# The attention loop of a hybrid transformer kernel: from the scheduler's order to a written order on four engines

## The chip, the cores and the metric

One core of a Trainium2 chip. The metric is device time of one execution in microseconds (us); a lower time is better. The engines are PE (matmuls; PEld is its weight load), DVE (vector), ACT (scalar, activations), POOL (GpSimd) and SP, which here only issues DMAs. Each engine works through its own queue of instructions in order and waits there, by semaphores, for the others.

## The reference, cut to what matters

Two layers of a hybrid backbone over 1,024 latent tokens and 256 context tokens of width 1,024. In each layer a normed input is projected once, the columns are split into attention heads, mLSTM heads and a pooling mixer, and the concatenation goes through one output projection; then a SwiGLU follows. The part that matters here is the attention: 8 query heads of 64, 2 key/value heads.

```python
def block_attention(q, k, v):
    ...
    def one_block(qi):                      # 128 queries
        s = jnp.einsum('bqhgd,bkhd->bhgqk', qi, k, preferred_element_type=F32) * scale
        p = jax.nn.softmax(s, -1).astype(v.dtype)
        return jnp.einsum('bhgqk,bkhd->bqhgd', p, v)
...
att_l = block_attention(q_l, jnp.concatenate([k_l, k_c], 1), jnp.concatenate([v_l, v_c], 1))
...
xl = xl + g1_l * (jnp.concatenate([att_l, ml_l, pool_l], -1) @ w_out)
```

In the first layer the 256 context tokens attend too, to themselves alone. All of it is 32-bit float.

## The kernel before

To keep 32-bit accuracy on 16-bit matmuls, an operand is split into an fp16 part and the fp16 remainder, and a product is three matmuls (`TERMS`). A split is an ACT copy and a subtraction on DVE or POOL.

The attention of a layer is a list of units. A unit is one head of one block of 128 queries against 1,280 keys; the blocks of context queries (first layer, two of them) have units of four heads against 256 keys. There are 68 units in layer 0 and 64 in layer 1. A unit passes through three methods:

- `front`: the scores, six matmuls into a tile `Sp` of three PSUM banks (there are two such tiles); the row maximum (`mx`, L1315, DVE); its scaling (L1320, or L1322 and L1323 for context units); the exponential on ACT into `pf` (two buffers), which also adds up the row's sum.
- `split`: the fp16 copy of `pf` into `phl` (three buffers), on ACT, in every eighth unit on DVE (L1334); the remainder on POOL (L169, the helper `tt`); the transpose of both by one DMA into `pT` (five buffers, L1340).
- `values`, for a pair of heads, that is two units: the reciprocal of the sums (L1351, DVE); two fp32 matmuls that spread it over the columns of a PSUM bank (L1354); an ACT copy of that into SBUF (`u`, tile `ao`); 60 value matmuls into other columns of the same bank (L1361); the scaling on DVE back into `ao`; an ACT copy to the fp16 part of `mixT` and a DVE subtraction for its remainder.

The loop (L1437) writes, in round i, `front` of unit i, `split` of unit i-1, at most one fill, and from round 5 on the values of units i-5 and i-4 where a pair begins; then `pump` takes one step of any running thread, such as a norm. A fill is a piece of the output projection: `w_get` brings a weight tile (the `w_split` inside it makes the split of the next tile: `hl`, an ACT copy and a DVE remainder), 12 matmuls for 256 or 512 tokens go into a PSUM bank (`wout`, L1372), and DVE adds the scaled result to `X`. `w_get` is called once for each of 24 weight tiles of a layer in the loop, and the tile serves one to three blocks of tokens. A budget decides when a fill is written: each round adds `pace`, a fill costs its tokens over 200.

```python
            if i >= 3:
                budget = min(budget + pace(i / nu), 3.0)
                if budget > 0:
                    c = next(fill, None)
                    if c is None:
                        c = next(fill_ffn, 0)
                    budget -= c
```

This text is not the order in which the engines run. A scheduler takes the instructions with their data dependencies, plays them through with costs of its own, and puts each on its engine's queue when it finds it ready; earlier text has the higher priority. Order edges that carry no semaphore can be added by `tc.add_manual_dep(..., order)`: the kernel does so for its activations, so that the table of functions is not switched back and forth (`after`), and for successive maxima (`tabs["mx"]`). PSUM in this stage is two `Sp` tiles of three banks and two single banks (`bank`), which the value pairs, the fills and the norms share in turn. The helpers `act` (L152), `stt` (L166) and `tt` (L169) issue most of the ACT, DVE and POOL work, so that rows carry their lines.

Of the kernel before, what the change touches and what calls it, by code (L numbers as in the profile page):

```python
# [9 lines left out]
F32 = mybir.dt.float32  # L10
# [8 lines left out]
P = 128  # L19
# [61 lines left out]
@with_exitstack  # L81
def hybrid_kernel(ctx: ExitStack, tc: tile.TileContext, I, out, dbg=None):
    nc = tc.nc
    V, S, G, TE, DMA = nc.vector, nc.scalar, nc.gpsimd, nc.tensor, nc.sync
    MUL, ADD, SUB, MAX, MIN = ALU.mult, ALU.add, ALU.subtract, ALU.max, ALU.min
    dbg = dbg or {}

# [33 lines left out]
    def bank3(name="S"):  # L121
        return cur["s"].tile([P, 1536], F32, tag="S", name=name)
# [5 lines left out]
    def pt_(shape, dt, tag, bufs=1, name=None):  # L128
        return cur["w"].tile(list(shape), dt, tag=tag, name=name or tag, bufs=bufs)

    def f2k(shape=(P, 512), dt=F32, name="f2k"):
        return pt_(shape, dt, "f2k", F2K[cur["kind"]], name)


    mm = TE.matmul
    order = mybir.DependencyInfo(mybir.DependencyClass.NoSync, mybir.DependencyReason.DATA)
    tabs = {"last": [], "pre": None, "kind": None}

    def after(i, j):
# [28 lines left out]
    def tt(o, a, b, op, e=None):  # L168
        (e or V).tensor_tensor(o, a, b, op=op)  # L169
# [354 lines left out]
    class Sums:  # L524


        def __init__(self, t0, n):
            self.t0, self.n, self.acc, self.k = t0, n, [], 0
# [212 lines left out]
    for l in range(DEPTH):  # L741
# [465 lines left out]
        for (t0, n) in BLOCKS:  # L1207
            if t0 in nx:
                drain(nx.pop(t0))
            for r in range(3):  # L1210
# [4 lines left out]
                else:  # L1215
                    pb = bank("pfm")
# [80 lines left out]
        class Unit:  # L1297
# [4 lines left out]

            def front(self):
                qt, nk, k0, n = self.qt, self.nk, self.k0, self.n
                Sp = bank3("Sp")
                for e, h in enumerate(self.hs):
                    ql = qkv[:, h // 2, h % 2, qt * P:(qt + 1) * P]
                    for a in range(2):
                        for b0 in range(0, nk, 512):
                            m = min(512, nk - b0)  # L1310
                            mm(Sp[:, e * nk + b0:e * nk + b0 + m], ql, qkv[:, 4 + h // 4, a, k0 + b0:k0 + b0 + m],  # L1311
                               start=(a == 0), stop=(a == 1), skip_group_check=True)
                ne = len(self.hs)
                mx = pt_((P, 4), F32, "mx", 3)
                r = V.tensor_reduce(mx[:, :ne], Sp[:, :n].rearrange("p (e k) -> p e k", e=ne), axis=AX.X, op=MAX)  # L1315
                if "mx" in tabs:
                    after(r.ins, tabs["mx"])
                h0 = self.hs[0]
                if ne == 1:
                    tabs["mx"] = V.tensor_scalar(mx[:, :1], mx[:, :1], rq[:, 1, qt, h0:h0 + 1], LN4096, op0=MUL, op1=ADD).ins  # L1320
                else:
                    tt(mx[:, :ne], mx[:, :ne], rq[:, 1, qt, h0:h0 + ne], MUL)  # L1322
                    tabs["mx"] = V.tensor_scalar(mx[:, :ne], mx[:, :ne], LN4096, None, op0=ADD).ins  # L1323
                self.pf = pt_((P, NTOK), F32, "pf", PFB)
                for e, h in enumerate(self.hs):
                    act(self.pf[:, e * nk:(e + 1) * nk], Sp[:, e * nk:(e + 1) * nk], AF.Exp, bias=mx[:, e:e + 1],
                        scale=rq[:, 0, qt, h:h + 1],
                        accum_out=self.qs[1][:, h:h + 1])

            def split(self):  # L1330
                i, n, pf = self.i, self.n, self.pf
                hl = pt_((P, 2, NTOK), F16, "phl", PHB)
                if i % 8 == 0:
                    V.tensor_copy(hl[:, 0, :n], pf[:, :n])  # L1334
                else:
                    act(hl[:, 0, :n], pf[:, :n])
                tt(hl[:, 1, :n], pf[:, :n], hl[:, 0, :n], SUB, G)
                self.pT = pt_((P, 2, 10, P), F16, "pT", PTB)
                if n == NTOK:
                    DMA.dma_start_transpose(out=self.pT.rearrange("p a k c -> p (a k) c"), in_=hl.rearrange("p a t -> p (a t)"))  # L1340
                else:
                    for a in range(2):
                        DMA.dma_start_transpose(out=self.pT[:, a, :n // P], in_=hl[:, a, :n])

        def values(us, pair):

            qt, sums = us[0].qt, us[0].qs[1]
            nkt, k0 = us[0].nk // P, us[0].k0
            hs = (2 * pair, 2 * pair + 1)
            kv = pair // 2  # L1350
            V.reciprocal(sums[:, hs[0]:hs[0] + 2], sums[:, hs[0]:hs[0] + 2])  # L1351
            pb = bank("pv")
            for g, h in enumerate(hs):
                mm(pb[64 * g:64 * g + 64, P:2 * P], sums[:, h:h + 1].to_broadcast([P, 64]), idn, start=True, stop=True)  # L1354
            u = f2k((P, 2, P), F32, "ao")
            act(u[:, 0], pb[:, P:2 * P])
            for kt in range(nkt):
                for j, (a, b) in enumerate(TERMS):
                    for g, h in enumerate(hs):
                        un = us[g if len(us) == 2 else 0]  # L1360
                        mm(pb[64 * g:64 * g + 64, 0:P], qkv[:, 6, b, k0 + kt * P:k0 + (kt + 1) * P][:, kv * 64:kv * 64 + 64],  # L1361
                           un.pT[:, a, un.hs.index(h) * nkt + kt], start=(kt == 0 and j == 0), stop=(kt == nkt - 1 and j == 2),
                           skip_group_check=True)
            tt(u[:, 1], pb[:, 0:P], u[:, 0], MUL)
            q = slice(qt * P, (qt + 1) * P)
            act(mixT[:, pair, 0, q], u[:, 1])
            tt(mixT[:, pair, 1, q], u[:, 1], mixT[:, pair, 0, q], SUB)

        def wout(w, k0, m, t0, n, pb):
            for k in range(4):  # L1370
# [62 lines left out]
        def pace(part):  # L1433

            return (1.1 if part < 0.9 else 2.5) if last else 0.8 if part < 0.2 else 1.5

        for i in range(nu + 5):  # L1437
            now[0] = i
            if i < nu:
                units[i].front()  # L1440
            if 1 <= i <= nu:
                units[i - 1].split()
            if i >= 3:
                budget = min(budget + pace(i / nu), 3.0)
                if budget > 0:
                    c = next(fill, None)
                    if c is None:
                        c = next(fill_ffn, 0)
                    budget -= c
            if i >= 5:  # L1450
                u = units[i - 5]
                if len(u.hs) > 1:
                    for e in range(0, len(u.hs), 2):
                        values([u], u.hs[e] // 2)
                elif u.hs[0] % 2 == 0:
                    values([u, units[i - 4]], u.hs[0] // 2)
                if u.hs[-1] in (6, 7) and u.qt < 8:
                    done[0] = u.qt
                units[i - 5] = u = None
            pump()  # L1460
        for _ in fill:
            pass
        units = fill = None
# [544 lines left out]
```

## Time and profile before

| | us |
|---|---|
| median of 3 runs | 2874.22 |
| lowest, highest | 2868.87, 2874.91 |
| the profiled execution | 2869.33 |
| its span, first to last instruction | 2867.5 |
| attention loop of layer 0, first score matmul to last exponential | about 373 to 704 |
| attention loop of layer 1 | about 1872 to 2160 |

The profile is one execution. An engine's busy time is the union of its instructions, and matmuls overlap each other, so that six matmuls of 0.4 us take 1.25 us together. A row's number in square brackets is the idle time of the engine ahead of it and what ended it. `issue` stands where nothing the profile shows was waited for. PEclk 1.00 is the full TensorE clock.

### The profile page before, as it was taken

How to read it: one execution, taken by the hardware profiler on the slowest of the kernel's cores; microseconds unless marked ns; L12 is line 12 of the kernel's file. 1: busy time of each engine (PE TensorE's matmuls, PEld its weight loads, DVE VectorE, ACT ScalarE, POOL GpSimd, SP SyncE). 2: the span in 40 equal slices, each digit the busy share in tenths (PEclk: the TensorE clock that was granted, in tenths of full speed). 3: DMA queues.
4: the chain of work that ended last, by engine and by line, in shares of the span. 5: the costliest groups of instructions: out<-in, count | busy, mean ns of one | idle time of the engine just before them, and what ended most of it. 6: DMA issues, size and time to landing. Idle time of an engine off the chain costs nothing. (4 is left out here: it accounts for less than half of the span.)

```text
span 2867.5 us, 54408 instructions
## 1 busy us (share of the span) xinstructions
PE 2601.2 (91%) x21619; PEld 1502.1 (52%) x21619; DVE 1951.8 (68%) x3379; ACT 1407.4 (49%) x2776; POOL 1283.6 (45%) x979
## 2 busy tenths in 40 slices
PE   7999978887889999999999998878877799999997
PEld 4875554555545555555554684544455344444444
DVE  5458867668766565656665567877778776666666
ACT  5345556666534343434344544466765444444453
POOL 1123445566434443444443213455664554555551
PEclk9999989999999999999999999999998899999999
DMA  9534487888122222222212212498984111111211
GB/s 291 151 108 128 134 191 141 154 149 171 52 74 82 81 89 89 82 81 89 74 45 76 67 53 68 123 173 160 171 168 106 45 59 52 59 59 45 67 52 74
DMA packets 631636, 296.28 MB, mean 103 GB/s; under 512 B 362888, under 2 KB 620756, under 8 KB 630868
## 3 DMA queue, kind: packets, MB, share of 16 engines
q1 hardware_dynamic: 631204, 292.73, 41.3%
q8 instruction: 169, 2.77, 0.4%
q14 instruction: 87, 0.71, 0.1%
q10 hardware_dynamic: 176, 0.07, 0.0%
HBM read 176.19 MB, written 20.87 MB: 69 GB/s over the span
## 5 line engine op out<-in xcount | busy, mean ns | idle before, releaser
L1903 PEld LDWEIGHTS <-hlp 128*128 128x128 f16 x5040 | 492.7, 98 | 609.7 <-issue 36.6
L1903 PE MATMUL Swb<-T,hlp 128*128 128x512 f16 x1920 | 446.2, 382 | 28.3 <-ACT T L152 14.3
L169 POOL TENSOR_TENSOR phl<-pf,phl 128x1280 f16<-128x1280 f32 (+1 forms) x132 | 345.2, 2617 | 260.9 <-ACT phl L152 160.3
L166 DVE SCALAR_TENSOR_TENSOR hlp<-ws,hlp 128x512 f16<-128x512 f32 (+1 forms) x320 | 235.2, 741 | 150.7 <-ACT hlp L152 116.7
L152 ACT ACTIVATE hlp<-ws 128x512 f16<-128x512 f32 (+1 forms) x320 | 163.7, 518 | 217.8 <-PE Swb L1903 86.7
L152 ACT ACTIVATE pf<-Sp,mx,rq 128x1280 f32<-128x1280 f32 (+1 forms) x144 | 189.8, 1320 | 142.1 <-DVE mx L1320 115.4
L1311 PE MATMUL Sp<-T 128*128 128x512 f16 (+1 forms) x800 | 180.9, 357 | 71.3 <-ACT pf L152 69.1
L1903 PE MATMUL Swc<-T,hlp 128*128 128x512 f16 x960 | 227.2, 379 | 0.0
L1903 PE MATMUL Swb<-tq,hlp 128*128 128x512 f16 x960 | 220.5, 379 | 4.9 <-ACT T L152 4.7
L1315 DVE TENSOR_REDUCE mx<-Sp 128x1 f32<-128x1280 f32 (+1 forms) x132 | 194.4, 1473 | 34.4 <-PE Sp L1311 34.0
L1372 PE MATMUL pwo<-T,hl 128*128 128x512 f16 (+1 forms) x960 | 190.6, 345 | 29.8 <-DVE X L166 11.6
L466 PE MATMUL pfm<-T,hl 128*128 128x512 f16 (+1 forms) x1032 | 213.6, 360 | 4.2 <-ACT E L152 4.1
L152 ACT ACTIVATE T<-sg 128x512 f16<-128x512 f32 (+1 forms) x170 | 100.2, 600 | 234.1 <-POOL sg L169 155.7
L166 DVE SCALAR_TENSOR_TENSOR hlp<-st,hlp 128x256 f16<-128x256 f32 (+1 forms) x201 | 142.5, 713 | 87.5 <-ACT hlp L152 73.0
L1915 PE MATMUL dx<-T,hlp 128*128 128x256 f16 x1440 | 177.9, 273 | 12.2 <-DVE hlp L166 6.4
L169 POOL TENSOR_TENSOR ws<-st 128x256 f32<-128x256 f32 (+1 forms) x97 | 103.0, 1069 | 183.5 <-DMA st<-in_w_ffn_down_dram 74.9
L169 POOL TENSOR_TENSOR X<-X,T 128x512 f32<-128x512 f32 x80 | 112.7, 1409 | 151.0 <-DVE X L166 112.2
L1903 PE MATMUL Swa<-T,hlp 128*128 128x512 f16 x720 | 169.1, 380 | 0.0
L1915 PEld LDWEIGHTS <-hlp 128*128 128x128 f16 x1440 | 139.2, 100 | 44.7 <-issue 10.8
L1361 PEld LDWEIGHTS <-T 128*64 128x64 f16 x3936 | 128.4, 119 | 56.4 <-issue 56.0
L152 ACT ACTIVATE hlp<-st 128x256 f16<-128x256 f32 (+1 forms) x201 | 101.3, 510 | 113.9 <-PE Swb L1903 71.1
L1361 PE MATMUL pv<-pT,T 128*64 128x128 f16 x3936 | 137.3, 233 | 17.6 <-ACT ao L152 17.5
(323 smaller groups left out, 4827.9 us busy)
## 6 DMA issues: line engine op xcount, KB each, us to landing
T<-in_w_ada_dram SPq DMA_DIRECT2D x48, 512.0 KB
rawa<-in_w_ada_dram SPq DMA_DIRECT2D x48, 512.0 KB
st<-in_w_in_dram SPq DMA_DIRECT2D x32, 512.0 KB
st<-in_w_out_dram SPq DMA_DIRECT2D x64, 256.0 KB
st<-in_w_ffn_gate_dram SPq DMA_DIRECT2D x32, 512.0 KB
st<-in_w_ffn_up_dram SPq DMA_DIRECT2D x30, 512.0 KB
st<-in_w_ffn_down_dram SPq DMA_DIRECT2D x30, 512.0 KB
xs<-X SPq DMA_DIRECT2D x4, 2048.0 KB
```

Source lines behind the costliest of these rows:

```text
L152: b = S.activation(o, i, f, **kw).ins
L166: V.scalar_tensor_tensor(o, a, s, b, op0=o0, op1=o1)
L169: (e or V).tensor_tensor(o, a, b, op=op)
L466: mm(o, w[:, a, k, :], h[:, k, b, t0:t0 + n], start=(k == 0 and j == 0), stop=(k == nk - 1 and j == 2))
L1311: mm(Sp[:, e * nk + b0:e * nk + b0 + m], ql, qkv[:, 4 + h // 4, a, k0 + b0:k0 + b0 + m], start=(a == 0), stop=(a == 1), skip_group_check=True)
L1315: r = V.tensor_reduce(mx[:, :ne], Sp[:, :n].rearrange("p (e k) -> p e k", e=ne), axis=AX.X, op=MAX)
L1361: mm(pb[64 * g:64 * g + 64, 0:P], qkv[:, 6, b, k0 + kt * P:k0 + (kt + 1) * P][:, kv * 64:kv * 64 + 64], un.pT[:, a, un.hs.index(h) * nkt + ...
L1372: mm(pb, w[:, a, k, :], mixT[:, k0 + k, b, t0:t0 + n], start=(k == 0 and j == 0), stop=(k == 3 and j == 2))
L1903: mm(o, w[:, a, k, :], B[:, b], start=(s in "172" and k == 0 and j == 0), stop=(k == kh(i) - 1 and j == 2), skip_group_check=True)
L1915: mm(dbank[i][:, r * 256:(r + 1) * 256], w[:, a, k, :], B[:, b], start=(first and k == 0 and j == 0), stop=(not first and k == kh(i) - 1 a ...
```

## The change

The engines of vector, scalar, GpSimd and tensor are wrapped in a class that, between `in_row(True)` and `in_row(False)`, adds an order edge from each instruction to the one written before it on the same engine. The loop runs inside that stretch, so its four queues have the order of the text; SP's queue has not. The text of a round is rewritten: values of units i-6 and i-5 come first, up to their matmuls; then `split` of unit i-1; then the scaling of these values; then `front` and the new `exps` of unit i; then fills, as many as the budget gives (it may grow to 4), but in a round with values only while it is above 2. The scaled values go to a third column range of the pair's PSUM bank instead of SBUF, and the two parts of `mixT` are made from there. All fp16 copies of `pf` are on ACT.

```diff
+    class InRow:
...
+            def call(*a, **k):
+                b = f(*a, **k)
+                if row["on"]:
+                    if self.key in row:
+                        tc.add_manual_dep(b.ins, row[self.key].name, order, reason="written order")
+                    row[self.key] = b.ins
+                return b
...
+    V, S, G, TE = (InRow(e, k) for k, e in enumerate((nc.vector, nc.scalar, nc.gpsimd, nc.tensor)))
...
+            def exps(self):
+                nk, qt, mx, Sp = self.nk, self.qt, self.mx, self.Sp
                 self.pf = pt_((P, NTOK), F32, "pf", PFB)
...
-                if i % 8 == 0:
-                    V.tensor_copy(hl[:, 0, :n], pf[:, :n])
-                else:
-                    act(hl[:, 0, :n], pf[:, :n])
+                act(hl[:, 0, :n], pf[:, :n])
...
-            u = f2k((P, 2, P), F32, "ao")
-            act(u[:, 0], pb[:, P:2 * P])
+            u = f2k((P, P), F32, "ao")
+            act(u, pb[:, P:2 * P])
...
-            tt(u[:, 1], pb[:, 0:P], u[:, 0], MUL)
+            yield
+            o = pb[:, 2 * P:3 * P]
+            tt(o, pb[:, 0:P], u, MUL)
             q = slice(qt * P, (qt + 1) * P)
-            act(mixT[:, pair, 0, q], u[:, 1])
-            tt(mixT[:, pair, 1, q], u[:, 1], mixT[:, pair, 0, q], SUB)
+            act(mixT[:, pair, 0, q], o)
+            tt(mixT[:, pair, 1, q], o, mixT[:, pair, 0, q], SUB)
...
-        for i in range(nu + 5):
+        in_row(True)
+        for i in range(nu + 6):
             now[0] = i
+            vals = []
+            if i >= 6:
+                u = units[i - 6]
+                if len(u.hs) > 1:
+                    vals = [values([u], h // 2) for h in u.hs[::2]]
+                elif u.hs[0] % 2 == 0:
+                    vals = [values([u, units[i - 5]], u.hs[0] // 2)]
...
+            for g in vals:
+                next(g)
+            if 1 <= i <= nu:
+                units[i - 1].split()
+            for g in vals:
+                next(g, None)
             if i < nu:
                 units[i].front()
-            if 1 <= i <= nu:
-                units[i - 1].split()
+            if i < nu:
+                units[i].exps()
             if i >= 3:
-                budget = min(budget + pace(i / nu), 3.0)
-                if budget > 0:
+                budget = min(budget + pace(i / nu), 4.0)
+                while budget > (2.0 if vals and i < nu else 0):
                     c = next(fill, None)
                     if c is None:
                         c = next(fill_ffn, 0)
+                    if not c:
+                        break
                     budget -= c
-            if i >= 5:
...
             pump()
+        in_row(False)
```

## Rows read from the trace of the kernel before

**Rows 1.** The page's parts 1 and 2: engines; DMA share in tenths by slice.

```profile
PE 2601.2 (91%) x21619; PEld 1502.1 (52%) x21619; DVE 1951.8 (68%) x3379; ACT 1407.4 (49%) x2776; POOL 1283.6 (45%) x979
...
DMA  9534487888122222222212212498984111111211
```

**Rows 2.** Windows, value rounds of the two loops, all engines.

```profile
core 0: us, PE busy (x) PEld busy (x) DVE busy (x) ACT busy (x) POOL busy (x), PEclk, DMA share, GB/s
395.40:705.00 309.60, 251.16 (x2914) 156.74 (x2913) 227.08 (x327) 198.53 (x331) 181.45 (x80) 0.94 0.83 154
1896.30:2160.00 263.70, 211.41 (x2533) 127.10 (x2530) 200.60 (x263) 177.19 (x264) 163.67 (x68) 0.94 0.91 168
```

**Rows 3.** The same windows, row maximum (L1315) alone.

```profile
395.40:705.00 309.60, 90.68 (x62) 0.94 0.83 154
1896.30:2160.00 263.70, 84.43 (x57) 0.94 0.91 168
```

**Rows 4.** Waits, layer 1 window: waiter, releaser, us, times, longest.

```profile
ACT pf L152 <- DVE mx L1320: 48.9, 20, 4.7
...
PE Sp L1311 <- ACT pf L152: 37.6, 24, 4.9
```

**Rows 5.** Tile ao, whole run: ns min/median/max; then who waited.

```profile
L169 DVE TENSOR_TENSOR T<-ao,T x72: 274/859/2667, 397.8 to 2178.6; 128x128 f16<-128x128 f32 x72
...
  PE pv L1361: 17.5, 20
```

**Rows 6.** Timeline, layer 1, 2020 to 2042 us: start, duration, instructions.

```profile
2022.85 0.44 PE L1354 MATMUL pv<-idn,sums 128*64 128x128 f32 x4
...
2023.22 0.93 PE L1311 MATMUL Sp<-T 128*128 128x512 f16 x4
...
2024.65 0.27 ACT L152 ACTIVATE ao<-pv 128x128 f32<-128x128 f32 x1
...
2024.96 1.87 PE L1361 MATMUL pv<-pT,T 128*64 128x128 f16 x60 [0.81 <-ACT ao L152]
...
2028.90 0.21 DVE L1320 TENSOR_SCALAR mx<-mx,rq 128x1 f32<-128x1 f32 x1
...
2029.23 1.42 ACT L152 ACTIVATE pf<-Sp,mx,rq 128x1280 f32<-128x1280 f32 x1 [1.65 <-DVE mx L1320]
...
2030.77 1.27 ACT L152 ACTIVATE phl<-pf 128x1280 f16<-128x1280 f32 x1
...
2037.78 2.62 POOL L169 TENSOR_TENSOR phl<-pf,phl 128x1280 f16<-128x1280 f32 x1 [0.27 <-POOL phl L169]
2038.08 2.47 DVE L169 TENSOR_TENSOR T<-ao,T 128x128 f16<-128x128 f32 x1
...
2038.36 1.25 PE L1311 MATMUL Sp<-T 128*128 128x512 f16 x6
```

**Rows 7.** Tile hl, 1896 to 2160 us.

```profile
L152 ACT ACTIVATE hl<-st x21: 612/618/630, 1910.6 to 2157.2; 128x512 f16<-128x512 f32 x21
L166 DVE SCALAR_TENSOR_TENSOR hl<-st,hl x20: 671/1399/3161, 1911.3 to 2157.7; 128x512 f16<-128x512 f32 x20
```

**Rows 8.** Tile X, 1896 to 2160 us.

```profile
L166 DVE SCALAR_TENSOR_TENSOR X<-pwo,prm,X x28: 467/739/751, 1897.9 to 2158.3; 128x512 f32<-128x512 f32 x22, 128x256 f32<-128x256 f32 x6
```

**Rows 9.** Line L1351, whole run.

```profile
L1351 DVE RECIPROCAL sums<-sums x72: 148/165/168, 380.4 to 2165.5; 128x2 f32<-128x2 f32 x72
```

**Rows 10.** Windows, two falls of the granted clock, before and behind each.

```profile
592.00:595.70 3.70, 0.80 (x8) 0.31 (x7) 3.61 (x6) 2.19 (x5) 0.36 (x1) 1.00 0.74 164
595.70:599.00 3.30, 3.30 (x61) 3.15 (x60) 0.17 (x1) 3.30 (x5) 2.22 (x1) 0.50 0.54 99
2086.00:2090.70 4.70, 0.33 (x2) 0.19 (x2) 3.32 (x8) 2.37 (x4) 1.32 (x2) 1.00 1.22 179
2090.70:2094.00 3.30, 3.30 (x11) 1.34 (x9) 3.30 (x3) 1.13 (x2) 2.30 (x1) 0.50 0.36 107
```

**Rows 11.** Timeline, layer 0, 511 to 520 us.

```profile
514.24 3.24 PE L1361 MATMUL pv<-pT,T 128*64 128x128 f16 x60 [1.74 <-ACT ao L152]
```

More of the change, by code (lines that the diff above doesn't have):

```diff
@@ L83, in hybrid_kernel, with __init__, __getattr__, in_row @@
     nc = tc.nc
-    V, S, G, TE, DMA = nc.vector, nc.scalar, nc.gpsimd, nc.tensor, nc.sync
+    order = mybir.DependencyInfo(mybir.DependencyClass.NoSync, mybir.DependencyReason.DATA)
+    row = {"on": False}
+    class InRow:
+        def __init__(self, e, key):
+            self.e, self.key = e, key
+        def __getattr__(self, name):
+            f = getattr(self.e, name)
+            def call(*a, **k):
[5 more added lines that the diff above has]
+                return b
+            return call
+    def in_row(on):
+        row.clear()
+        row["on"] = on
+    V, S, G, TE = (InRow(e, k) for k, e in enumerate((nc.vector, nc.scalar, nc.gpsimd, nc.tensor)))
+    DMA = nc.sync
     MUL, ADD, SUB, MAX, MIN = ALU.mult, ALU.add, ALU.subtract, ALU.max, ALU.min
@@ L135, in hybrid_kernel @@
     mm = TE.matmul
-    order = mybir.DependencyInfo(mybir.DependencyClass.NoSync, mybir.DependencyReason.DATA)
     tabs = {"last": [], "pre": None, "kind": None}
@@ L1304, in front @@
                 qt, nk, k0, n = self.qt, self.nk, self.k0, self.n
-                Sp = bank3("Sp")
+                Sp = self.Sp = bank3("Sp")
                 for e, h in enumerate(self.hs):
@@ L1323, in front @@
                     tabs["mx"] = V.tensor_scalar(mx[:, :ne], mx[:, :ne], LN4096, None, op0=ADD).ins
+                self.mx = mx
+            def exps(self):
+                nk, qt, mx, Sp = self.nk, self.qt, self.mx, self.Sp
                 self.pf = pt_((P, NTOK), F32, "pf", PFB)
+                self.mx = self.Sp = None
                 for e, h in enumerate(self.hs):
@@ L1435, in pace @@
             return (1.1 if part < 0.9 else 2.5) if last else 0.8 if part < 0.2 else 1.5
-        for i in range(nu + 5):
+        in_row(True)
+        for i in range(nu + 6):
             now[0] = i
+            vals = []
[5 more added lines that the diff above has]
+                    vals = [values([u, units[i - 5]], u.hs[0] // 2)]
+                if u.hs[-1] in (6, 7) and u.qt < 8:
+                    done[0] = u.qt
+                units[i - 6] = u = None
+            for g in vals:
[4 more added lines that the diff above has]
+                next(g, None)
             if i < nu:
                 units[i].front()
-            if 1 <= i <= nu:
-                units[i - 1].split()
+            if i < nu:
+                units[i].exps()
             if i >= 3:
-                budget = min(budget + pace(i / nu), 3.0)
-                if budget > 0:
+                budget = min(budget + pace(i / nu), 4.0)
+                while budget > (2.0 if vals and i < nu else 0):
                     c = next(fill, None)
@@ L1448, in hybrid_kernel @@
                         c = next(fill_ffn, 0)
+                    if not c:
+                        break
                     budget -= c
-            if i >= 5:
[L1451 to L1459, printed above, removed]
             pump()
+        in_row(False)
         for _ in fill:
```

## The prediction

> **What bounds the kernel now.** I read the page's first two parts first [rows 1]: PE is busy 91% of the span, but in slices 6 to 10 and 27 to 30 of the forty, where the two attention loops lie, the DMA row stands at 7 to 9 and is low almost everywhere else. The rest of the program is not touched, so the argument is about those two stretches. Next the windows of the two loops [rows 2], taken from the round at which values begin: 309.6 us in layer 0 and 263.7 us in layer 1. No engine is full there: PE 81% and 80%, DVE 73% and 76%, ACT 64% and 67%, POOL 59% and 62%; the DMA engines, with the transposes of the probabilities, are at 0.83 and 0.91. The row-maximum line counted in the same windows gives the pace [rows 3]: 62 units in 309.6 us and 57 in 263.7 us. As two units make a head pair with one `values`, that is 31 pairs at 9.99 us and 28.5 pairs at 9.25 us. Third, who waits for whom [rows 4]: the exponentials (`pf`) wait 48.9 us for the scaled maximum, and `Sp` waits 37.6 us for exponentials. So the loop is bound by nothing single; it is a ring of waits PE, DVE, ACT, which the scheduler loosens by letting PE run one or two score tiles ahead of the values.
>
> **What the new order fixes.** A round with values runs, on each engine in this order: reciprocal (DVE), two broadcasts (PE), copy `u` (ACT), 60 value matmuls (PE); fp16 copy of unit i-1 (ACT), its remainder (POOL), transpose; scaling (DVE), two parts of `mixT` (ACT, DVE); scores of unit i (PE), maximum and its scaling (DVE), exponential (ACT); then fills. The next round has no values.
>
> Three of these edges close a ring. The value matmuls wait for `u`, which lies in the same bank: 20 times PE idled until it was done, 17.5 us in all [rows 5]; one is shown, `u` at 2024.65, matmuls at 2024.96 [rows 6]. The scores of unit i now stand behind those matmuls on PE. And `u` stands behind the previous round's exponential on ACT. Before, scores ran first: 2023.22 ahead of 2024.96 [rows 6].
>
> **The ring for one pair, step by step** (from the timeline [rows 6]; the maximum is 84.43 us over 57 [rows 3]):
> - `u` 0.27, 60 value matmuls 1.87, six score matmuls 1.25, maximum 1.48, scaling 0.21, exponential with its accumulator read 1.54 (it starts at 2029.23, the next ACT instruction at 2030.77): 6.62 us;
> - next round: fp16 copy 1.27, exponential 1.54 (its scores and maximum ran meanwhile): 2.81 us;
> - hand-overs between engines as the timeline shows them, 0.03 to 0.12 us each: 0.42 us.
>
> That is 9.85 us. 31 pairs make 305 us against 309.6 (-4), 28.5 make 281 against 263.7 (+17): together **+13 us**. The first six rounds, where the loads of `X` dominate, and what follows the loop I leave as they are.
>
> **Weight tiles.** `w_get` in a fill emits, behind the round's exponential, an fp16 copy `hl` on ACT (0.62) and its remainder on DVE (0.67 at least, 1.40 in the median) [rows 7]. Behind the remainder on DVE stands the fill's update of `X` (0.74, or 0.47 for 256 tokens [rows 8]), and behind that the next reciprocal (0.16 [rows 9]), for which the broadcasts (0.44 [rows 6]) and then `u` wait. Before, these could be put where there was room; now `u` starts later by 0.62 + 0.7 + 0.74 + 0.16 + 0.44 and hand-overs 0.2 = 2.9 us, or 3.1 where POOL is still at its 2.62 us remainder. I take 3.0; with the median remainder it would be 3.6, 21 us more in 35 pairs. A non-weight fill costs nothing: its matmuls follow the scores and end some 2 us before `u`, its update of `X` lies beside the second exponential; with that cover gone it would cost its 0.74. Following the budget (pace 0.8, 1.5, 1.1, 2.5; a cost of tokens/200; fills held back in a value round) through both layers, 30 rounds of the steady stretch hold one `w_get`; five more near the end hold 2, 2, 3 and 4, 4. 30 times 3.0 is 90. In the other five each further tile adds its copy, remainder and update, 0.62 + 0.7 + 0.47, 1.9 with hand-overs: 4.9 + 4.9 + 6.8 + 8.7 + 8.7 = 34. Together **+124 us**. The lower bound is nothing, if these copies found room elsewhere; the edges exclude a gain.
>
> **TensorE's clock.** The granted clock falls to 0.50, the 1.2 GHz level, behind stretches in which PE idled for 2.9 and 4.4 us; two such pairs of stretches are shown [rows 10]. A pass of values at that level takes 3.24 us instead of 1.87 [rows 11]. In the new round PE has nothing but 0.44 us of broadcasts from the end of the fill to the values: 2.5 us, and 5 to 6 us where a weight tile is split. I take the low clock for the 35 weight pairs and half of the other 24.5: 47 times 1.37 is **+64 us**. Bounds: none (+0), and every pair with values and scores both doubled (59.5 times 1.37 + 1.25, +156). By the Trainium skill, TensorE: Matmul & The Clock Gate, HAM oscillation, idle stretches between bursts of matmuls make every burst start cold; the trace agrees for the bursts shown. By that rule alone all 59.5 pairs would pay 1.37, 82 us, and the sum would be 18 us higher.
>
> **Scaled values through PSUM, every unit by ACT, the rest.** The remainder of `mixT` takes 0.27 us at least but 0.86 in the median and up to 2.67 [rows 5]; one of 2.47 us ends with POOL's 2.62 [rows 6]. No row has it reading PSUM; the nearest is ACT's copy `u` out of the same bank, 0.27 [rows 6]. I take 0.28; the upper bound is today's median. By the Trainium skill, SBUF — State Buffer, Who interferes with whom, a DVE operation with two SBUF inputs is shut out while GpSimd reads SBUF and one with a PSUM input is not; the trace agrees so far as `X` updates, which read PSUM, never exceed 0.75 [rows 8]. At 0.28 instead of 0.86 DVE gets 0.6 us back per pair, but beside the scores (1.25 us), which the maximum waits for anyway: with a blocked remainder the maximum would be some 0.8 us late, so I count nothing, and +48 us at worst, 0.8 in every pair. The eighth of the copies that moves from DVE to ACT (1.27) is in the ring already. Values a round later hold `pT` longer: five slots, the sixth needed just after the value matmuls, before POOL's remainder is done; the transposes, issued from SP, wait for that remainder and not for the slot. Norm steps put in the row near the end: up to 15 us, not counted.
>
> **Sum.** 13 + 124 + 64 = +201 us. The profiled execution took 2869.33 us (its span 2867.5 and 1.8 around it), within the three runs and 5 us under their median; 2869 + 201 = **3070 us**.
>
> **Rivals.** *The ring alone* (weight tiles hidden, clock held): 2869 + 13 = 2882 us. For it: the clock is 0.94 in the loops today; against it: the instruction order on DVE. *Faster, the round runs at the rate of the transposes:* if the values did not have to wait for `u`, or PE got the scores out first, ACT (0.64, 0.67) and DVE would have room, and the limit would be the DMA share: 309.6 times 0.17 and 263.7 times 0.09 saved, 53 + 24 = 77, so 2792 us. For it: the waits [rows 4] and the blocked remainders, which a fixed order does away with. It decides from the point where a pair takes less than 9.6 us, today's mean of both; against it, 9.85 without one delay. *The edges do not bind* and the scheduler's order stays: 2869 us; against it, the existing order edges among activations are made the same way.
>
> **How the numbers follow.** Forecast 0.72 (own range 2960 to 3180), ring alone 0.14 (2870 to 2930), faster 0.10, no effect 0.04. A measurement of this kernel tells about 0.2% (6 us) from no change. The ring alone touches that bound, but most of it lies above: faster 0.11, same 0.04, slower 0.85. The range takes in most of the ring alone below and the doubled clock price above: 2885 to 3180 us.
>
> **What would show it.** The maximum-line should have a pace of 9.8 us a pair where no weight tile is split and near 13 where one is; PE's first value matmul right behind `u` in every pair, with `u` behind an exponential; `Sp` no longer waiting for exponentials but standing behind the values; `u` waiting for the broadcasts in weight rounds; more stretches at 0.50 in the loops; the `mixT` remainder at 0.28; DMA share near 0.7. It is wrong if the pairs stay under 9.3 us, above all if value matmuls start before `u` ends, or if the scores are found ahead of the values on PE.

## The result, and the profile after

The changed kernel takes 3130.43 us in the median of four runs (3125.30 to 3132.85), the kernel before 2872.98 on the same chip: a ratio of 1.0896, 95% interval 1.0876 to 1.0916. The forecast was 3070, 201 us more than the profiled run before; measured were 257 us more. The profiled execution spans 3126.5 us, against 2867.5.

The page of the kernel after (part 1, the DMA share of part 2, one group of part 5; nearly all lines are L96 now, that of the wrapper):

```profile
PE 2674.6 (86%) x21619; PEld 1566.6 (50%) x21619; DVE 1851.3 (59%) x3362; ACT 1433.5 (46%) x2793; POOL 1279.2 (41%) x979
...
DMA  8534565656322222222212212766655112212111
...
L96 PE MATMUL Sp<-T 128*128 128x512 f16 (+1 forms) x800 | 170.3, 365 | 8.7 <-ACT pf L96 6.9
```

PE is busy for 73 us more than in [rows 1], at the same number of matmuls. The DMA row, which stood at 7 to 9 in the loops, stands at 5 to 7. The scores now wait 6.9 us for exponentials in the whole run; before it was 37.6 us in one layer's window [rows 4].

The windows of the two loops, all engines (columns as in [rows 2]):

```profile
395.40:807.00 411.60, 279.27 (x2898) 185.00 (x2895) 174.21 (x305) 205.81 (x328) 176.35 (x77) 0.84 0.61 114
2020.00:2406.00 386.00, 240.21 (x2580) 156.62 (x2581) 164.38 (x264) 194.26 (x281) 168.49 (x71) 0.85 0.62 120
```

The windows are 33% and 46% longer than in [rows 2] and hold about the same work. DVE is busy for a fifth less, PE for 11 and 14% more, ACT for 4 and 10% more; the granted clock has gone from 0.94 to 0.84 and 0.85, and the DMA share from 0.83 and 0.91 to 0.61 and 0.62. Nothing became full; the ring of waits became longer.

Counted between the starts of exponentials, the loss can be split. The first six rounds took 6 us more (in both layers together). From the seventh exponential to the last it was 302.3 and 261.3 us before and 401.8 and 374.5 after: +213 us. From the end of a layer's last exponential to the first FFN gate product `Swb` (layer 0) or to the end of the run (layer 1) it was 111.5 and 708.3 before, 136.8 and 720.8 after: +38 us. Together 257.

The waits of layer 1's loop after the change (waiter, releaser, us, times, longest us):

```profile
PE pv L96 <- DVE sums L96: 96.8, 28, 5.2
...
ACT pf L96 <- DVE mx L96: 72.5, 30, 3.4
...
PE pv L96 <- ACT ao L96: 26.9, 29, 2.3
```

The broadcasts wait 96.8 us for the reciprocals of 28 pairs. That wait is the new one, and most of it comes from weight tiles: 78 us are the waits of 5.2 us in the fifteen rounds with one tile; the plain pairs have 1.0 to 2.5 us each. The timeline shows why. First a pair without a weight tile, layer 1 (start, duration, engine, instructions, idle time before and its releaser):

```profile
2047.81 0.26 ACT L96 ACTIVATE ao<-pv 128x128 f32<-128x128 f32 x1
...
2048.12 1.87 PE L96 MATMUL pv<-pT,T 128*64 128x128 f16 x60 [1.20 <-ACT ao L96]
...
2049.92 2.34 PE L96 MATMUL Sp<-T 128*128 128x512 f16 x12
...
2050.74 0.29 DVE L96 TENSOR_TENSOR T<-pv,T 128x128 f16<-128x128 f32 x1 [0.34 <-ACT T L96]
2051.21 1.49 DVE L96 TENSOR_REDUCE mx<-Sp 128x1 f32<-128x1280 f32 x1 [0.18 <-PE Sp L96]
...
2053.07 1.42 ACT L96 ACTIVATE pf<-Sp,mx,rq 128x1280 f32<-128x1280 f32 x1 [2.36 <-DVE mx L96]
...
2054.61 1.27 ACT L96 ACTIVATE phl<-pf 128x1280 f16<-128x1280 f32 x1
...
2055.79 1.40 ACT L96 ACTIVATE pf<-Sp,mx,rq 128x1280 f32<-128x1280 f32 x1
...
2057.18 0.26 ACT L96 ACTIVATE ao<-pv 128x128 f32<-128x128 f32 x1
...
2057.50 3.20 PE L96 MATMUL pv<-pT,T 128*64 128x128 f16 x60 [2.33 <-ACT ao L96]
```

The ring is there link by link: `u` behind the exponential, the values 0.05 us behind `u`, the scores of two rounds (x12) behind the values, the maximum as soon as its scores are there, then the exponential, the fp16 copy, the second exponential and the next `u`. From `u` to `u` it is 9.37 us. The second pass of values, at 2057.50, takes 3.20 us instead of 1.87; the window around it has a granted clock of 0.54 (columns as above):

```profile
2057.40:2060.60 3.20, 3.10 (x60) 3.03 (x59) 0.00 (x0) 1.20 (x2) 3.09 (x2) 0.54 0.35 67
```

Now a weight tile between two pairs, the same timeline some 10 us later:

```profile
2066.72 2.61 POOL L96 TENSOR_TENSOR phl<-pf,phl 128x1280 f16<-128x1280 f32 x1 [5.38 <-ACT phl L96]
...
2067.89 0.62 ACT L96 ACTIVATE hl<-st 128x512 f16<-128x512 f32 x1
2068.54 1.34 DVE L96 SCALAR_TENSOR_TENSOR hl<-st,hl 128x512 f16<-128x512 f32 x1 [3.23 <-ACT hl L96]
2069.80 0.74 DVE L96 SCALAR_TENSOR_TENSOR X<-pwo,prm,X 128x512 f32<-128x512 f32 x1
2070.46 0.15 DVE L96 RECIPROCAL sums<-sums 128x2 f32<-128x2 f32 x1
...
2070.76 0.70 PE L96 MATMUL pv<-idn,sums 128*64 128x128 f32 x4 [5.20 <-DVE sums L96]
...
2071.49 0.28 ACT L96 ACTIVATE ao<-pv 128x128 f32<-128x128 f32 x1 [2.98 <-PE pv L96]
```

`u` could have started at 2067.89, right behind the exponential's read of its accumulator. It starts 3.60 us later: copy 0.62, remainder 1.34, update of `X` 0.74, reciprocal 0.15, broadcasts 0.70 at the low clock (0.50 granted from 2070.70 to 2071.50, after PE had been idle for 5.20 us), and 0.05 of hand-overs beyond the overlaps.

The remainder of the weight tile in layer 1's loop (ns least, median, most):

```profile
L96 DVE SCALAR_TENSOR_TENSOR hl<-st,hl x24: 675/1334/1339, 2034.5 to 2396.1; 128x512 f16<-128x512 f32 x22, 128x1024 f16<-128x1024 f32 x2
```

In all fifteen rounds with one tile it takes 1.33 us, since in the written order it there follows the exponential after which POOL is still at its own remainder: above, POOL's runs from 2066.72 to 2069.33 and DVE's from 2068.54 to 2069.88. The other nine lie in the last rounds, with no such remainder of POOL beside them; the seven of 512 columns take 0.68 to 0.82.

### The profile page after: what moved, and what is told of

It is laid out like the page before. It is cut to its first block, busy times and chain, and to the rows that moved or that the text cites. A ratio compares the mean times of both kernels' runs of the same rounds, so it can differ in the third digit from the quotient of the medians.

```text
span 3126.5 us, 54484 instructions
## 1 busy us (share of the span) xinstructions
PE 2674.6 (86%) x21619; PEld 1566.6 (50%) x21619; DVE 1851.3 (59%) x3362; ACT 1433.5 (46%) x2793; POOL 1279.2 (41%) x979
## 3 DMA queue, kind: packets, MB, share of 16 engines
q1 hardware_dynamic: 631204, 292.73, 37.6%
## 5 line engine op out<-in xcount | busy, mean ns | idle before, releaser
L96 PEld LDWEIGHTS <-hlp 128*128 128x128 f16 x6768 | 660.3, 99 | 677.9 <-issue 71.2
L96 POOL TENSOR_TENSOR phl<-pf,phl 128x1280 f16<-128x1280 f32 (+1 forms) x132 | 342.7, 2596 | 486.9 <-ACT phl L96 364.3
L96 PEld LDWEIGHTS <-T 128*64 128x64 f16 (+1 forms) x7520 | 402.3, 126 | 163.0 <-issue 109.4
L96 PE MATMUL Swb<-T,hlp 128*128 128x512 f16 x1920 | 445.0, 381 | 28.9 <-ACT T L96 13.7
L96 PEld LDWEIGHTS <-hl 128*128 128x128 f16 x2424 | 241.9, 102 | 282.0 <-issue 79.8
L96 DVE SCALAR_TENSOR_TENSOR hlp<-ws,hlp 128x512 f16<-128x512 f32 (+1 forms) x320 | 228.8, 721 | 148.9 <-ACT hlp L96 121.0
L96 ACT ACTIVATE pf<-Sp,mx,rq 128x1280 f32<-128x1280 f32 (+1 forms) x144 | 189.3, 1316 | 170.3 <-DVE mx L96 162.3
L96 ACT ACTIVATE hlp<-ws 128x512 f16<-128x512 f32 (+1 forms) x320 | 163.6, 518 | 215.0 <-PE Swb L96 88.3
L96 PE MATMUL pv<-pT,T 128*64 128x128 f16 x3936 | 184.4, 275 | 60.5 <-ACT ao L96 60.5
L96 PE MATMUL Swc<-T,hlp 128*128 128x512 f16 x960 | 227.2, 379 | 0.0
L96 PE MATMUL Swb<-tq,hlp 128*128 128x512 f16 x960 | 220.5, 379 | 3.6 <-ACT T L96 3.6
L96 PE MATMUL pwo<-T,hl 128*128 128x512 f16 (+1 forms) x960 | 190.0, 353 | 36.0 <-DVE X L96 15.6
L96 PE MATMUL pfm<-T,hl 128*128 128x512 f16 (+1 forms) x1032 | 218.1, 365 | 2.6 <-ACT E L96 2.4
L96 DVE TENSOR_REDUCE mx<-Sp 128x1 f32<-128x1280 f32 (+1 forms) x132 | 195.1, 1478 | 30.8 <-PE Sp L96 30.8
L96 ACT ACTIVATE T<-sg 128x512 f16<-128x512 f32 (+1 forms) x170 | 100.3, 600 | 232.1 <-POOL sg L96 155.0
L96 PE MATMUL pv<-idn,sums 128*64 128x128 f32 x288 | 40.2, 362 | 190.5 <-DVE sums L96 186.0
L96 DVE SCALAR_TENSOR_TENSOR hlp<-st,hlp 128x256 f16<-128x256 f32 (+1 forms) x201 | 140.9, 705 | 90.7 <-ACT hlp L96 76.0
L96 DVE TENSOR_TENSOR pv<-pv,ao 128x128 f32<-128x128 f32 x72 | 21.5, 299 | 287.3 <-PE pv L96 231.8
L96 PE MATMUL dx<-T,hlp 128*128 128x256 f16 x1440 | 177.3, 273 | 8.2 <-ACT hlp L96 8.2
L96 POOL TENSOR_TENSOR ws<-st 128x256 f32<-128x256 f32 (+1 forms) x97 | 102.8, 1068 | 183.7 <-DMA st<-in_w_ffn_down_dram 70.4
L96 PE MATMUL Sp<-T 128*128 128x512 f16 (+1 forms) x800 | 170.3, 365 | 8.7 <-ACT pf L96 6.9
L96 POOL TENSOR_TENSOR X<-X,T 128x512 f32<-128x512 f32 x80 | 112.7, 1409 | 146.3 <-DVE X L96 112.2
```

Source lines behind the costliest of these rows:

```text
L96: b = f(*a, **k)
```

## The experiments

The kernel before was run beside them on the same chip, with a median of 2873 us each time; ratios are to it, with their 95% intervals.

**The edges alone.** `e1_no_edges`: the text of after, but the scheduler orders the loop.

```diff
-        in_row(True)
+        in_row(False)
```

> The changed text with the order edges left out: the scheduler orders the four engines as before. My theory (the edges close a ring from the copy u over value matmuls, scores, maximum and two exponentials): the loops fall back to about the old pace, 9.2 to 10 us a pair, and the kernel takes 2830 to 2900 us. Rival, the text itself costs (values a round later, fills kept out of value rounds, scaled values in PSUM): most of the 257 us stays, over 3000 us.

Measured: 2821.07 us, ratio 0.9823 (0.9808 to 0.9838). So the new text is 52 us faster than before, and the edges cost 309 us. The windows of its two loops, which last 297 and 260 us (columns as in [rows 2]):

```profile
400.00:674.00 274.00, 235.80 (x2808) 145.75 (x2807) 179.39 (x302) 199.51 (x325) 173.68 (x76) 0.97 0.91 166
1872.00:2113.00 241.00, 204.25 (x2476) 121.83 (x2475) 167.24 (x259) 185.23 (x272) 165.99 (x70) 0.97 1.00 184
```

The DMA share is at 0.91 and 1.00, the clock at 0.97. That fits the rival "faster", in which the transposes set the pace; no run varied the transposes alone, so that they are the limit is argued, not shown. What in the text gives the 52 us was asked twice, from both sides.

**Scaled values through PSUM, alone.** `e8_before_scaled_in_psum` is the kernel before with this one edit, after which both parts of `mixT` are made from `o`; `e11_no_edges_sbuf` is `e1_no_edges` with the scaled values back in SBUF.

```diff
-            tt(u[:, 1], pb[:, 0:P], u[:, 0], MUL)
+            o = pb[:, 2 * P:3 * P]
+            tt(o, pb[:, 0:P], u, MUL)
...
```

> The kernel before with one part of the change alone, the scaled values in PSUM. Theory, this part is what the text gains (the text without edges took 2821 us, 52 less than before): the mixT remainder at 0.29 us in place of 0.86 in the median, DVE free for the maximum, 2825 to 2860 us. Rival, the gain comes from the other parts (values a round later, the fill rule, copies all on ACT): 2865 to 2880 us.

> The changed text without edges and with the scaled values in SBUF. If the place of the scaled values is the whole gain of the text (2873 to 2821; the kernel before with that part alone took 2823), this returns to 2865 to 2885 us. If the rest of the text gains of itself, below 2860 us.

Measured: 2823.40 us, ratio 0.9832 (0.9817 to 0.9847), and 2865.53 us, ratio 0.9974 (0.9965 to 0.9983). The one edit is worth 50 us on the old text and 44 on the new one; all the rest of the new text is worth 8. The row that explains it is the remainder of `mixT`, first in `e8_before_scaled_in_psum` (groups by form: count, busy us, mean ns, idle before):

```profile
L169 DVE TENSOR_TENSOR T<-pv,T 128x128 f16<-128x128 f32 x72 | 20.4, 285 | 20.2 <-ACT T L152 20.1
```

and in `e11_no_edges_sbuf` (ns least, median, most, as in [rows 5]):

```profile
L96 DVE TENSOR_TENSOR T<-ao,T x72: 264/586/2733, 400.4 to 2182.6; 128x128 f16<-128x128 f32 x72
```

Reading PSUM it takes 0.29 us in the mean of all 72, and at most 0.293, though 43 of them run beside a remainder on POOL; reading SBUF it takes up to 2.73. By the Trainium skill, SBUF — State Buffer, Who interferes with whom, a DVE instruction with two SBUF inputs contends with a GpSimd instruction that reads SBUF, one with at most one SBUF input does not; these rows agree. What it costs is seen in the exponentials' wait for their scaled maximum (`pf` for `mx`, as in [rows 4], from the first to the last exponential of each layer): 122 us in the two loops before, 81 in `e8_before_scaled_in_psum`; 108 in `e11_no_edges_sbuf`, 62 in `e1_no_edges`. The remainder of 2.47 us in [rows 6], from 2038.08 on, stands on DVE between a maximum and its scaling, which starts only as it ends:

```profile
2040.47 0.20 DVE L1320 TENSOR_SCALAR mx<-mx,rq 128x1 f32<-128x1 f32 x1
```

**The same edit undone under the edges.** `e4_scaled_in_sbuf`: after, with the scaled values in SBUF.

```diff
-            o = pb[:, 2 * P:3 * P]
+            o = u2[:, 1]
```

> The edges kept, the scaled values back in SBUF as before the change. By the prediction the mixT remainder is hidden beside the scores: no change when counted at nothing, up to 48 us more (3178 us) if POOL's subtraction blocks it in every pair and the maximum comes late. Its duration should rise from 0.29 us to over 1 us in the mean. Rival, reading and writing PSUM is the dearer way: under 3120 us.

Measured: 3156.79 us, ratio 1.0983 (1.0963 to 1.1002), 26 us above after. Its remainder, in the columns of the last row:

```profile
L96 DVE TENSOR_TENSOR T<-ao,T x72: 292/293/2657, 403.7 to 2474.1; 128x128 f16<-128x128 f32 x72
```

52 of the 72 are undisturbed and 18 take over 0.4 us; the mean is 0.62, where over 1 was expected. Where one is held up it stands ahead of the maximum on DVE: a plain pair then has 7.5 us between exponentials instead of 6.7, a round with context units 9.5 to 10.0 instead of 7.8 to 8.4.

**The scores first.** `e2_scores_first`: after, with `front` of unit i written ahead of the values, the exponential where it was.

```diff
+            if i < nu:
+                units[i].front()
             for g in vals:
                 next(g)
...
-                units[i].front()
-            if i < nu:
```

> The edges kept, front of unit i written ahead of the values, so that the scores no longer stand behind the value matmuls on PE; the reciprocal then stands behind the maximum of unit i. Ring theory: values and scores leave the chain of a pair, which by the same durations becomes about 8.1 us where no weight tile is split (9.4 measured) and about 12 where one is (13.5 to 15 measured); 3000 to 3070 us. Rival, the loss lies in the weight tiles and the clock alone and the place of the scores is indifferent: 3115 to 3145 us.

Measured: 3107.09 us, ratio 1.0806 (1.0779 to 1.0833). My theory had 3000 to 3070 and missed; the rival, 3115 to 3145, is nearer but was not met either. The timeline, layer 1, shows which link is left:

```profile
2055.64 0.21 DVE L96 TENSOR_SCALAR mx<-mx,rq 128x1 f32<-128x1 f32 x1
2055.77 0.16 DVE L96 RECIPROCAL sums<-sums 128x2 f32<-128x2 f32 x1
...
2057.13 3.41 PE L96 MATMUL pv<-pT,T 128*64 128x128 f16 x60 [0.36 <-ACT ao L96]
...
2060.64 0.30 DVE L96 TENSOR_TENSOR pv<-pv,ao 128x128 f32<-128x128 f32 x1 [4.72 <-PE pv L96]
...
2060.98 0.28 ACT L96 ACTIVATE T<-pv 128x128 f16<-128x128 f32 x1 [2.74 <-DVE pv L96]
...
2061.15 1.41 ACT L96 ACTIVATE pf<-Sp,mx,rq 128x1280 f32<-128x1280 f32 x1
```

The scaled maximum of unit i is there at 2055.85, but on ACT its exponential stands behind the fp16 part of `mixT` (2060.98), which stands behind the scaling, which waits for the values. Besides, the reciprocal now also stands behind this maximum (2055.77). The 23 us are what is left of two effects: in layer 1, 27 of 29 passes of values take over 2.2 us here, in after 20, so the clock costs more. The two plain pairs that have their values in 1.87 us have 6.8 us between exponentials, no less than the 6.7 of after.

**PE left out of the edges.** `e12_pe_free`: edges on DVE, ACT and POOL alone.

```diff
-                if row["on"]:
+                if row["on"] and self.key != 3:
```

> The changed kernel with edges on DVE, ACT and POOL, none on PE. Ring theory: the scheduler lets scores go ahead of the value matmuls, the maximum no longer waits for them, plain pairs fall from 9.4 us to 8 us or less; what stays is the weight tiles' remainder ahead of the reciprocal on DVE (84 us by the run with the reciprocal ahead): 2900 to 3020 us. Rival, the value parts reach the exponential through ACT all the same (the fp16 part of mixT stands ahead of it), so PE's order alone is worth little, as in the run with the scores first: 3060 to 3130 us.

Measured: 3107.03 us, ratio 1.0811 (1.0796 to 1.0827): again 23 us, as the rival had it. Its timeline, layer 1:

```profile
2058.82 0.30 DVE L96 TENSOR_TENSOR pv<-pv,ao 128x128 f32<-128x128 f32 x1 [3.92 <-PE pv L96]
2059.15 0.28 ACT L96 ACTIVATE T<-pv 128x128 f16<-128x128 f32 x1 [2.02 <-DVE pv L96]
2059.46 0.29 DVE L96 TENSOR_TENSOR T<-pv,T 128x128 f16<-128x128 f32 x1 [0.34 <-ACT T L96]
2059.67 1.48 DVE L96 TENSOR_REDUCE mx<-Sp 128x1 f32<-128x1280 f32 x1
...
2061.49 1.42 ACT L96 ACTIVATE pf<-Sp,mx,rq 128x1280 f32<-128x1280 f32 x1 [2.06 <-DVE mx L96]
```

The values' scaling, its two parts, the maximum, the exponential: DVE and ACT keep them in a line. Here too the 23 us are a balance: the weight pairs have mostly 9.8 to 12.1 us between exponentials, and only 10 of 29 passes of layer 1 take over 2.2 us, but most plain pairs have 8.3 us instead of 6.7, since the scheduler puts products of the output projection ahead of their values on PE: in one `u` ends at 2065.86 and the values start at 2067.79, behind six of them.

**The reciprocal ahead of the weight tile.** `e3_reciprocal_ahead`: after, but the next pair's reciprocal is written ahead of the fills.

```diff
             V.reciprocal(rr, rr)
+            yield
...
+            ahead = pairs(i + 1)
+            for g in ahead:
+                next(g)
             if i >= 3:
```

> The edges kept; only the reciprocal of the next pair is written a little earlier, in front of the fills instead of behind them. Weight-tile theory: the broadcasts need not wait for the remainder of hl and the update of X, a weight pair loses all but the copy hl on ACT (0.65 us) of its 4.6 us over a plain one, 35 times 3.5 is 120 us less: 2980 to 3040 us, plain pairs still 9.4. Rival, the weight pairs are long for another reason (late weight loads, the low clock, ACT): under 30 us less, over 3100 us.

Measured: 3045.96 us, ratio 1.0605 (1.0590 to 1.0621): 84 us below after, not 120, and just above the range expected. In the first half of layer 1's loop a weight pair now has mostly 7.2 us between exponentials, 0.5 over a plain one. In the second half it has 7.7 to 10.3, and the timeline shows two causes:

```profile
2219.51 0.62 ACT L96 ACTIVATE hl<-st 128x512 f16<-128x512 f32 x1
2220.03 0.62 ACT L96 ACTIVATE sq<-X 128x512 f32<-128x512 f32 x1
...
2220.55 0.26 ACT L96 ACTIVATE ao<-pv 128x128 f32<-128x128 f32 x1
...
2220.87 3.28 PE L96 MATMUL pv<-pT,T 128*64 128x128 f16 x60 [3.19 <-ACT ao L96]
```

The square of a norm step (`sq`, 0.62) also stands ahead of `u` on ACT, and the values run at the low clock, 3.28.

**The clock kept up.** `e5_clock_kept_up`: `e3_reciprocal_ahead` with nine matmuls per pair ahead of the broadcasts, whose result is overwritten.

```diff
+            for _ in range(9):
+                mm(pb, id16, qkv[:, 4, 0, 0:512], start=True, stop=True, skip_group_check=True)
```

> The kernel with the reciprocal ahead, and nine more matmuls of 512 columns per pair whose result is overwritten, in front of the broadcasts, where PE idles 2.2 to 2.8 us before the values. Clock theory: the value passes of 3.2 to 3.4 us become 1.87 us, some 30 pairs lose 1.4 us each, about 40 us less than that kernel's 3046 us: 2990 to 3020 us, with the granted clock near 1.00 in the loops. Rival, the slow passes cost nothing or the nine matmuls only add work: 3040 to 3120 us.

Measured: 3038.03 us, ratio 1.0581 (1.0563 to 1.0599): only 8 us less, and the intervals of the two ratios overlap. Layer 1's steady window, first of `e3_reciprocal_ahead`, then of `e5_clock_kept_up`:

```profile
1996.00:2322.00 326.00, 224.75 (x2502) 144.08 (x2500) 159.80 (x257) 185.42 (x271) 161.59 (x68) 0.89 0.74 136
```

```profile
1990.00:2316.00 326.00, 274.18 (x2872) 159.44 (x2870) 168.14 (x269) 192.90 (x279) 169.74 (x72) 0.96 0.78 145
```

and of the latter's timeline the added matmuls and the values of the pair that answers to the one shown above:

```profile
2213.14 2.10 PE L96 MATMUL pv<-T,id 128*128 128x512 f16 x9
...
2216.98 1.86 PE L96 MATMUL pv<-pT,T 128*64 128x128 f16 x60 [1.37 <-ACT ao L96]
```

The clock rises from 0.89 to 0.96, the values take 1.86 us, and the weight pairs of the second half have 7.7 us between exponentials. Layer 1's loop gains 14 us (352.6 to 338.5). Layer 0's loses 10 (399.0 to 409.3): its four rounds with context units, which have two pairs and so eighteen added matmuls, take 41 us between exponentials instead of 32, and six of its later weight rounds 0.7 to 2.3 us more each. The added matmuls stand ahead of the values on PE and hold one of the two banks. So the price of the low clock in a pass is shown; that it can be had back as a whole is not.

**The edges ended with the last unit.** `e6_edges_to_last_unit`:

```diff
+            if i == nu:
+                in_row(False)
```

> The changed kernel with the order edges ended at the round of the last unit, so that the six rounds that only finish values, fills and norms are ordered by the scheduler. Theory of the tails (of the 257 us, 25 lie between layer 0's last exponential and its FFN loop and 13 behind layer 1's, since those rounds too stand in line): 20 to 40 us less, 3090 to 3110 us. Rival, the tails are longer because work was left over, whatever the order: 3125 to 3135 us.

Measured: 3105.04 us, ratio 1.0815 (1.0796 to 1.0833): 25 us less. By the profiles 31 of the 38 us behind the loops come back, 15 or 16 in each layer, and layer 1's loop takes 4 us more. In layer 0 the last values end 23.7 us behind the last exponential, in after 38.1, since there a weight copy that waits 4.90 us for its load, the norm steps and the FFN's first products stand in one row with them.

**Scores a round ahead, exponential ahead of the scaling, reciprocal ahead of the fills.** `e7_scores_a_round_ahead` keeps the edges and cuts every link of the ring; `e9_ahead_to_last_unit` also ends them with the last unit; `e10_ahead_one_fill` also takes the old rule of at most one fill a round. The text of a round:

```python
            for g in vals: next(g)            # broadcasts, u
            if i + 1 < nu: units[i + 1].front()
            for g in vals: next(g)            # values
            if 1 <= i <= nu: units[i - 1].split()
            if i < nu: units[i].exps()
            for g in vals: next(g, None)      # scaling, mixT
            ahead = pairs(i + 1)              # then: reciprocal, fills
```

> The edges kept, another written order: scores and maximum of unit i+1 in round i, between u and the value matmuls; the scaling of the values behind the exponential; the reciprocal ahead of the fills. Ring theory: no chain runs any more from u over values, scores and maximum to the exponential of the same round; a pair is then held by PE's own 7.6 us (broadcasts 0.44, values 1.87, scores 2.5, a fill 2.75) or ACT's 6.2 to 7.2, so 7.6 to 8.3 us a pair, DMA share back near 0.9: 2780 to 2860 us. Rival, any fixed order loses against the scheduler's on this loop: over 2950 us.

> The order with scores a round ahead (2852 us), and the order edges ended at the last unit's round. The tail theory of the earlier run (25 us for that edit on the changed kernel) gives 2820 to 2835 us. Rival, with the loop shorter the tails are bound by the norms themselves: 2845 to 2855 us.

> The same, with the old fill rule, at most one fill in a round and in value rounds too. In the run with scores a round ahead each layer ends with two rounds of 16 us that hold three or four fills, against 8 us a pair elsewhere. If those rounds cost their fills' chains, 10 to 25 us less than the kernel with the fills in bursts: 2800 to 2820 us, level with the scheduler's order on the same text (2821). Rival, fills in value rounds delay the values and cost more than they save: over 2835 us.

Measured: 2851.51 us, ratio 0.9926 (0.9912 to 0.9941); 2833.07, ratio 0.9858 (0.9845 to 0.9870); 2847.32, ratio 0.9908 (0.9896 to 0.9921). The first two as expected: with the edges on all four engines the kernel is now 0.7 and 1.4% faster than before. The third missed and its rival was right: the old rule is 14 us slower than `e9_ahead_to_last_unit`, not faster, and the loss lies in the loops, 582 us against 561 for both. The timeline of the first, layer 1, a round with a weight tile:

```profile
2043.18 1.24 PE L96 MATMUL Sp<-T 128*128 128x512 f16 x6 [0.23 <-ACT pf L96]
...
2044.07 0.26 ACT L96 ACTIVATE ao<-pv 128x128 f32<-128x128 f32 x1
...
2044.39 1.87 PE L96 MATMUL pv<-pT,T 128*64 128x128 f16 x60
...
2045.39 1.41 ACT L96 ACTIVATE pf<-Sp,mx,rq 128x1280 f32<-128x1280 f32 x1
...
2047.25 0.29 DVE L96 TENSOR_TENSOR pv<-pv,ao 128x128 f32<-128x128 f32 x1
```

Scores run ahead of `u` (2043.18) and the exponential of unit i runs beside the values (2045.39); only the scaling stands behind both (2047.25). The windows of its loops:

```profile
400.00:672.00 272.00, 240.05 (x2842) 148.39 (x2836) 181.09 (x304) 196.52 (x323) 172.76 (x76) 0.94 0.90 167
1885.00:2134.00 249.00, 216.17 (x2566) 130.05 (x2561) 161.41 (x259) 185.29 (x275) 166.00 (x70) 0.92 0.99 183
```

The DMA share is 0.90 and 0.99, as in `e1_no_edges`: the loops last 295 and 268 us against 297 and 260 there. It stays 30 us behind `e1_no_edges`; by the profiles 6 lie in the loops and 25 behind them (last exponential to `Swb`, or to the end). No version with edges beat the two without: 2821.07 and 2823.40 us, whose runs overlap.

## Why the prediction came out as it did

**What the new order fixes: right.** Every edge named is in the timeline: values right behind `u`, `u` behind the previous exponential, `Sp` behind the values and no more waiting for exponentials. That these edges are the cause is shown by `e1_no_edges` (309 us) and by `e7_scores_a_round_ahead`, where the same engines keep an order of the text without this ring and 279 us come back, 194 of them beyond what the earlier reciprocal alone gives in `e3_reciprocal_ahead`. That the chain closes elsewhere when one link is cut is shown by the timelines of `e2_scores_first` and `e12_pe_free`; their 23 us each are no clean price of a link, as the clock and PE's order changed with it. The DMA share, said to be near 0.7, came to 0.61 and 0.62.

**The ring, 9.85 us a pair: 9.4.** ACT's next instruction starts some 0.1 us before the last one's end, which my sum of durations did not have, and the scores start before the modelled end of the values. In layer 1, which has no context units, the 57 steps behind the seventh exponential would be 265.9 us at 2.7 and 6.7 us each (29 and 28 of them), against 261.3 before: +5 where I had +17.

**Weight tiles, 3.0 us: 3.6, the value that I gave for the median remainder.** There were 30 rounds with one tile, as forecast; 29 of them stand ahead of values. Those have 11.7 us between exponentials in the median, 5.0 more than a plain one: 3.6 by the timeline for the late `u`, the rest for values at the low clock. In layer 1 the fifteen such rounds cost 76.2 us, the last two, with 4 and 5 tiles, 26.7 (forecast 17 for two rounds of 4; the steps behind them are counted in), and the ring 4.6; with the low clock in four plain pairs (8.0 to 8.2 instead of 6.7 us), 5.6 us, that is the whole of its 113. Layer 0 lost 100 in the same way, but its rounds with context units, long before and after, are not so easily told apart.

**The clock, 1.37 us a pass: right.** The 1.4 us that the weight rounds cost beyond the late `u`, and 1.3 to 1.5 in the plain pairs it touched, are that price, and `e5_clock_kept_up` takes it away in all but 3 of layer 1's 29 passes. In the plain pairs I had it in half of them; in layer 1 it was 4 of 11. Of the 58 full passes of both layers, 41 take over 2.2 us, 55 us in all above 1.87 (forecast 47 and 64); 10 such passes, 14 us, were there before, which my sum did not take off. Not every burst behind idle time paid: the pass at 2048.12, behind 1.20 us, takes 1.87, the one at 2057.50, behind 2.33 us, 3.20.

**That the loops came so near is in part luck.** They were forecast at +201 from the seventh exponential on and came to +213. By the prediction's own prices layer 1 would have lost 110 us, an estimate: ring 17, fifteen rounds with one tile 45, two with four tiles 17, and 31 for the clock in 17 weight pairs and half of 11.5 plain ones. It lost 113: ring 4.6, late `u` 53.9 (fifteen times 3.59), the last two rounds 26.7, and 27.9 that I put down to the low clock. The ring was 12 too dear and the tiles 18 too cheap.

**What follows the loop, left as it is: the step that failed.** It cost 38 us, the largest part of the 56 between forecast and measured loss, and the first six rounds 6. I had the norm steps near the end at up to 15 us and did not count even these; but the row ends with the loop's last round, so six rounds of values, weight copies and FFN products were also held in the order of the text. `e6_edges_to_last_unit` gives back 31 of the 38 there.

**Scaled values through PSUM, counted as nothing: wrong for the kernel before, nearly right inside the ring.** Alone it is worth 50 us, as much as the +48 that I gave as the worst case the other way round: a blocked remainder did delay the scaled maximum there, as the waits of 122 and 81 us show. Under the edges it is worth 26. My sum of the ring had the remainder at 0.28 and hidden, and so it is (0.29); but the change should have been seen as a gain of some 50 and edges that cost 309.

**The rivals.** "Ring alone" fell with the weight tiles. "The edges do not bind" fell with `e1_no_edges`. "Faster at the rate of the transposes" described `e1_no_edges` and `e7_scores_a_round_ahead` well: DMA share 0.90 to 1.00, loops 56 and 49 us shorter than before, where it said 77. It had the condition right, too: scores ahead of the values. That this alone is not enough, because the exponential must also stand ahead of the scaling, I did not see, and `e2_scores_first` taught it.

**Open.** How the loss of `e5_clock_kept_up` in layer 0 divides between PE's time and the held bank, and by which wait one fill a round is slower in `e10_ahead_one_fill`, was not separated. Of the 7 us behind the loops that `e6_edges_to_last_unit` does not give back no run tells the cause. No run took the edges off DVE, ACT or POOL alone.

## What to carry to other kernels

Before writing an order for several engines, follow each instruction's queue once around: two instructions of different threads that are neighbours on one engine become a dependency, and a loop of such neighbours sets the pace. Here two cuts of a single link gave 23 us each and all cuts together 279, so look for the path that is left before trying one cut. Put short instructions that release another engine (here a reciprocal of 0.15 us) ahead of long ones that nobody waits for, start the next round's producers before this round's consumers, and end the order where the steady loop ends. Try each part of a change by itself: here one small edit was worth 50 us and was buried under edges that cost 309.

## What the runs showed of the hardware

The remainder of `mixT` read from PSUM took 0.27 to 0.29 us in all 72 cases of `e8_before_scaled_in_psum`, 43 of them beside a remainder on POOL; with both operands in SBUF it took up to 2.73, and this one edit was worth 44 and 50 us of 2870 without the edges. Nine added matmuls of 512 columns ahead of the broadcasts took the granted clock of layer 1's loop from 0.89 to 0.96 and the pass of values shown from 3.28 to 1.86 us, and yet the run gained no more than 8 us of 3046.
